# Half of the state groups in one recurrence, and all of its preparation on VectorE, in an MLA + S5 backbone

## The chip, the cores and the metric

The kernel runs on one core of a Trainium2 chip. The metric is the device time of one execution in microseconds (us). Five engines work side by side, each through its own list of instructions in order: TensorE (PE, with its weight loads PEld), VectorE (DVE), ScalarE (ACT), GpSimd (POOL) and SyncE (SP), which issues nearly all the DMAs.

## The reference, cut to what matters

Two post-norm layers over 512 latent tokens and 256 context tokens, 1024 features, float32. Layer 0 is latent attention and is not touched. Layer 1 is a bidirectional S5 state-space layer with a GLU:

```python
u_l, g_l = jnp.split(h_lat @ w_in, 2, axis=-1)      # also for the context
# per direction, per group (128 groups of 16 channels, 64 complex states):
#   state[t] = lam_bar * state[t-1] + b_bar u[t];   y[t] = Re(C state[t])
# first over the context, then, from its last state, over the latent tokens
y = jax.nn.gelu(d * u + y_forward + y_backward)
ya, yb = jnp.split(y @ w_glu + b_glu, 2, axis=-1)
out = ((ya * sigmoid(yb)) * silu(g)) @ w_out        # then residual and LayerNorm
```

## The kernel before, in words

Products with weights run as three float32r matmuls on parts: weights and inputs are split into a high part (`whi`, cast on ACT) and the rest (`wlo`, a subtraction on DVE, line 64).

Tokens are taken in chunks of 8: 64 chunks of latent tokens and 32 of context. Both directions of 64 states lie on the 128 partitions. Layer 1 has these stages, and `m` (0 to 15) counts pieces of 128 channels, which are 8 groups:

- **Stage A** (18 turns of the loop at line 1154). Turn t projects the channels of m = t (`u_tile`: 24 matmuls of 512 columns and 24 of 256), writes them to DRAM (`ud`) in one layout and reads them back in another (`u_load`). `s_tile(m)`, two turns later, makes each chunk's input to the state with 16 groups of matmuls of 96 columns, from weights `pt` (`win_chunk`). Of 32 pieces of such weights 24 were made ahead and are loaded; 8 late ones (pieces 5, 8, ... 26) are made here, by six operations on POOL (lines 372 to 377) out of two loads. ACT copies the results to `st` and, for the context, to `sc`. `tree(k)`, after every second m, folds the 32 context chunks of 16 groups into one state by five levels of four operations, on POOL (lines 1123 to 1128).
- **The recurrence** (`recur`, lines 1131 to 1142) turns inputs into states: 63 steps one after the other, each of four operations (lines 1138 to 1141) on all 32 groups of a quarter of the groups, that is 64 numbers a partition, each 256 bytes from the next. Three quarters run on DVE and the last one on POOL. A quarter can start when its two trees are done. `pull(n)` emits n steps of the recurrences that are open, between other work.
- **Stage B**: the gates (a projection, tanh and product, `gg`, stored to `gd`), and for each m `y_load` (state-out weights `wo`, lag table `toe`, `u`), `states` (copies of the states on ACT), `y_tile` (matmuls of 128 columns) and the copy `ot` on DVE. `gelu(n)` turns two of these and makes the GLU's inputs. y_tile(m) needs the finished recurrence of its groups.
- **GLU, output projection, norm**: matmuls in a row, with the weights loaded and split as they go.

What one writes down is not the order that the engines get: a scheduler of the framework places each engine's instructions. Each engine then runs its list in order, so an instruction that waits holds up all behind it. SP's list has the weight loads (`wraw`, which wait for the subtraction that frees their buffer), the loads of `pt`, `bt`, `u`, `toe`, `wo` and the stores of `gd` in one row.

Of the kernel before, what the change touches and what calls it, by code (L numbers as in the profile page):

```python
# [31 lines left out]
def hybrid_mla_s5(ctx, tc, I, O):  # L32
# [55 lines left out]
    def mod_steps(blocks, wt, ps, work, n):  # L88
        """rows of 512 columns of the modulation, block j in column group j: one step for each of the inputs' tiles"""
# [48 lines left out]
    def newton_rsqrt(y, t, ms):  # L138
        """y = 1/sqrt(ms), with one Newton step"""
        act.activation(y, ms, AF.Abs_reciprocal_sqrt)  # L140
        dve.tensor_mul(t, y, y)
        dve.tensor_mul(t, t, ms)
        dve.tensor_scalar(t, t, -0.5, 1.5, op0=ALU.mult, op1=ALU.add)
        dve.tensor_mul(y, y, t)
# [14 lines left out]
    def s5_params(take, mm):  # L159
# [102 lines left out]
        # (lam_bar - 1) / lam  # L262
# [16 lines left out]
        # powers: slot s holds lam_bar^s forward, lam_bar^(7-s) backward; state-in coefficients  # L279
        # coef * lam_bar * slot(7 - i), groups on the partitions, conjugated  # L280
# [33 lines left out]
    def s5_chunk(work, mm, c, pw, cci, half, dcol, eyek):  # L314
        """state-out weights and lag tables of groups 4c .. 4c+3"""
# [16 lines left out]
        # input weights of the lag table, the directions in separate columns  # L332
# [48 lines left out]
    def win_early(tables, scratch, engs, more):  # L381
        """pieces made ahead and kept in DRAM: the last one is stored, the next one loaded, this one made"""
# [13 lines left out]
    # ================= layer 0: latent attention =================  # L396
    with ExitStack() as ctx_:
# [25 lines left out]
        def turn_rows(dst, src):  # L423
            """the features that the rotation pairs: blocks of 16 rows change places"""
            for i in range(8):
                sp.dma_start(out=dst[16 * i:16 * i + 16, :], in_=src[16 * (i ^ 1):16 * (i ^ 1) + 16, :])

        def stack(src, dst0, dst1, sl):
            """hi and lo of two heads' 64 rope features, one over the other"""
# [77 lines left out]
        with mkpool(name="in_h", bufs=KC) as hp, mkpool(name="in_w", bufs=3) as wp, \  # L507
# [20 lines left out]
            def mod_part(q):  # L528
                """shift and scale of 256 features, the even and the odd tiles of the inputs apart"""
# [74 lines left out]
            def rms(tiles, cols, n):  # L604
                """RMSNorm over the partitions of the tiles, in place"""
# [86 lines left out]
            def mod_more():  # L692
                """a step of the products with the modulation weights, and the loads for the next one"""
# [19 lines left out]
        with mkpool(name="at_s", bufs=2) as work, mkpool(name="at_p", bufs=2, space=PSUM) as ps, \  # L713
# [7 lines left out]
            # a unit is 128 latent queries of a head, or its 256 context queries  # L721
# [36 lines left out]
            def turn(i):  # L758
                """probabilities with the keys on the partitions, split"""
# [51 lines left out]
            for i, (h, u) in enumerate(units + [(HEADS, 0), (HEADS, 0)]):  # L811
# [19 lines left out]
                if i == len(units) - 8:  # L831
                    # the first operands of the output projection
# [27 lines left out]
    def norm_cols(work, st):  # L860
        """mean and 1/std of rows from the statistics of their pieces"""
# [6 lines left out]
    # PSUM from here on: four tiles of a bank, and two of two banks  # L868
# [66 lines left out]
    def res_load(tt, n):  # L935
        """gate and residual of a token tile, for half of the features"""
# [35 lines left out]
    # the weights in the order of their use, 1024 columns at a time, two pieces ahead  # L972
# [25 lines left out]
    with mkpool(name="o_s", bufs=1, side="right") as work:  # L998
# [19 lines left out]
        def modulated(tt, z):  # L1018
            """input of layer 1, feature-major, split"""
# [29 lines left out]
    def win_chunk(c):  # L1049
# [6 lines left out]
        win_make(pool, pt, bt, *(winp.tile([P, 4, P], F32, name=f"t{i}", bufs=1) for i in range(2)))  # L1056

    # ================= layer 1: S5 =================
    ud = [dram.tile([8, P, 96], F32, name=f"ud{m}") for m in range(16)]
    gd = [dram.tile([P, TL], F32, name=f"gd{m}") for m in range(16)]  # L1060
    stes, (stp,) = pools(dict(name="st", bufs=4))
    ST = [stp.tile([P, 2, 32, 64], F32, name="st") for _ in range(4)]      # states: (re, -im), group, chunk
# [20 lines left out]
    def s_tile(m):  # L1083
        """state inputs of the groups of an m: in the order of each direction's steps"""
# [19 lines left out]
    def lam(l, gs, tail):  # L1104
        """the power's real part, and (+,-) its imaginary part, for (re, -im) states"""
# [7 lines left out]
    def tree(k):  # L1113
        """state after the context, for 16 groups"""
        x = scs.pop(k)
        gs = slice(16 * k, 16 * k + 16)
        for l in range(5):
# [5 lines left out]
            pool.tensor_tensor(a, ev, lr, op=ALU.mult)  # L1123
            pool.tensor_tensor(b, ev[:, ::-1], li, op=ALU.mult)
            pool.tensor_tensor(a, a, b, op=ALU.add)
            g = slice(16 * k % 32, 16 * k % 32 + 16)
            dst = a if l < 4 else ST[k // 2][:, :, g, 0:1]
            pool.tensor_tensor(dst, a, od, op=ALU.add)
            x = a

    def recur(q, work, eng):
        """states before each chunk of the latent tokens, for 32 groups, in steps"""
        st = ST[q]
        lr, li = lam(0, slice(32 * q, 32 * q + 32), 0)
        for k in range(63):
            t1 = work.tile([P, 2, 32], F32, name="rt1", bufs=4)
            t2 = work.tile([P, 2, 32], F32, name="rt2", bufs=4)
            eng.tensor_tensor(t1, st[:, :, :, k], lr, op=ALU.mult)  # L1138
            eng.tensor_tensor(t2, st[:, ::-1, :, k], li, op=ALU.mult)  # L1139
            eng.tensor_tensor(st[:, :, :, k + 1], st[:, :, :, k + 1], t1, op=ALU.add)  # L1140
            eng.tensor_tensor(st[:, :, :, k + 1], st[:, :, :, k + 1], t2, op=ALU.add)  # L1141
            yield
# [11 lines left out]
    for t in range(18):  # L1154
# [10 lines left out]
        if m >= 0:  # L1165
            s_tile(m)
            pull(3)
            if m % 2 == 1:
                tree(m // 2)
            if m % 4 == 3 and m < 15:  # L1170
                rec.append(recur(m // 4, stp, dve))
# [20 lines left out]
    yes, (ep,) = pools(dict(name="y_s", bufs=2, side="right"))  # L1192
    rec.append(recur(3, stp, pool))
    toe, ins = {}, {}

    def y_load(m):
# [5 lines left out]
        wo = [ep.tile([P, 4, 2, P], F32, name="wo", bufs=5) for _ in range(2)]  # L1202
        for c in range(2):
            sp.dma_start(out=wo[c], in_=wod[2 * m + c])
        u = ep.tile([P, 8, 96], F32, name="u", bufs=3)
# [5 lines left out]
    def states(m):  # L1211
        """the states of 8 groups; the backward half was made in the order of its steps: turn it round"""
# [5 lines left out]
    def y_tile(m):  # L1218
        """two groups at a time in the halves of the columns, chunks on the partitions"""
# [11 lines left out]
        if m % 2 == 0:  # L1231
            ot[m // 2] = ep.tile([P, 8, 2, 64], F32, name="ot")
# [5 lines left out]
    def gelu(n):  # L1238
        """channels of two tiles turned onto the partitions; tanh form, split"""
# [4 lines left out]
        for e in range(2):  # L1244
# [7 lines left out]
            h, l = (VV[v // 4][:, v % 4, i] for i in range(2))  # L1252
# [23 lines left out]
    gates(6, gg)  # L1276
    states(0)
    gates(1, gg)
    for m in range(16):
# [3 lines left out]
        pull(4)  # L1283
        if m < 15:
            states(m + 1)
        if "gggggggg.g.a.aaa"[m] == "g":
            gates(1, gg)
        elif "gggggggg.g.a.aaa"[m] == "a":
            glu_mm()
        if m % 4 == 2:  # L1290
            VV.append(stp.tile([P, 4, 2, TL], F32R, name="st"))
        if m % 4 >= 2:
            gelu(m // 2 - (m % 2 == 0))
# [26 lines left out]
    with mkpool(name="f_s", bufs=1, side="right") as work:  # L1320
# [25 lines left out]
        wlast = [stp.tile([P, 2, 2, D], F32R, name="st") for _ in range(4)]  # L1346
# [32 lines left out]
def tables():  # L1379
# [9 lines left out]
    cs = np.stack([cos, sin * sgn], 1)[tok]          # [512, 2, 64]  # L1389
# [4 lines left out]
def lay_out(inp):  # L1394
# [13 lines left out]
    def mtiles(w):                                     # [K, M] -> [M/128, 128 p, K/128 * 128]  # L1408
# [7 lines left out]
    uk, uv = g["mla_w_uk"][0], g["mla_w_uv"][0]        # [128 c, 16, 128]  # L1416
# [5 lines left out]
    def dp(a):                                         # [2, 128 g, 64 p, ...] -> [(d p), g, ...]  # L1422
# [48 lines left out]
```

## Time and profile before

| what | before |
|---|---|
| runs shown, us | 1840.08, 1853.53, 1857.38 |
| median | 1853.53 |
| span of the profiled execution | 1848.7 |
| PE busy / DVE busy / POOL busy in the span | 1653.3 / 1137.1 / 683.2 |
| TensorE clock granted, mean | 0.944 |

The page gives no time of the profiled execution beside its span; the span lies inside the three times. Starts are counted from the span's start. Layer 1's stage A takes about 962 to 1218 us, stage B 1218 to 1412, the rest the remaining 436 us.

### The profile page before, as it was taken

To read this page: it belongs to the slowest core of one execution; us is meant where nothing else is said; L and a number is where in the kernel's file an instruction comes from. 1 tells how busy PE (TensorE), PEld (TensorE's weight loads), DVE (VectorE), ACT (ScalarE), POOL (GpSimd) and SP (SyncE) were. 2 spreads that over 40 slices of the span, in tenths; PEclk is the share of its full clock that TensorE was granted. 3 is DMA by queue.
4 is the path that set the end of the run, shared out by engine and by line. 5 is a ranking of instruction groups with operands and counts; after the bars stand their busy time and mean duration, and the time that the engine had idled before them with its cause. 6 is when DMAs were issued, how large, how long until landed. Compare 5 with 4: busy or idle time off the path is not lost.

```text
span 1848.7 us, 26973 instructions
## 1 busy us (share of the span) xinstructions
PE 1653.3 (89%) x9754; PEld 1321.5 (71%) x9754; DVE 1137.1 (62%) x2356; ACT 694.6 (38%) x1415; POOL 683.2 (37%) x788
## 2 busy tenths in 40 slices
PE   7999998888988989987899875687979999999997
PEld 4755787766766767766779765565768888888876
DVE  3864448888899677735551499998844332333347
ACT  2511226465565646611334332233454222222220
POOL 0000017666776477445105664626770000000022
PEclk8999999899999989998999887888989999999999
DMA  9366412222222455467647755339995333333352
GB/s 324 99 211 203 112 52 88 74 92 83 85 70 90 136 164 166 145 204 219 202 133 211 165 134 153 119 91 266 258 288 156 129 108 105 112 98 119 105 180 68
DMA packets 144244, 268.82 MB, mean 145 GB/s; under 512 B 39760, under 2 KB 74848, under 8 KB 143984
## 3 DMA queue, kind: packets, MB, share of 16 engines
q1 hardware_dynamic: 126256, 258.69, 46.9%
q10 hardware_dynamic: 17792, 8.39, 1.6%
q8 instruction: 77, 1.26, 0.3%
q14 instruction: 55, 0.45, 0.1%
q0 software_dynamic: 64, 0.03, 0.0%
HBM read 215.39 MB, written 49.30 MB: 143 GB/s over the span
## 4 chain that ended last, share of the span: by engine, by line
PE 53%; DVE 21%; DMA 14%; ACT 3%; issue 3%; POOL 3%; SPq 1%; DVEq 0%; ACTq 0%; POOLq 0%
PE mm L80 13%; PE mm L81 13%; PE mm L82 13%; DMA wraw<-in_wout_dram 3%; DVE st L1141 3%; DVE rt L1138 3%; DMA pt<-pind 3%; DVE st L1140 2%; DVE rt L1139 2%; PE modps L102 2%; PE sc L739 2%; PE sc L738 2%; DVE wlo L64 2%; DMA toe<-kd 2%; PE tr L775 2%
## 5 line engine op out<-in xcount | busy, mean ns | idle before, releaser
L64 DVE TENSOR_TENSOR wlo<-wraw,whi 128x1024 fp32r<-128x1024 f32 (+1 forms) x155 | 184.2, 1190 | 349.1 <-ACT whi L64 347.8
L64 ACT CAST whi<-wraw 128x1024 fp32r<-128x1024 f32 (+1 forms) x155 | 148.9, 962 | 467.5 <-PE mm L81 302.9
L81 PE MATMUL mm<-st,whi 128*128 128x512 f32 x512 | 201.6, 394 | 0.0
L80 PE MATMUL mm<-st,whi 128*128 128x512 f32 x512 | 201.3, 393 | 0.4 <-DVE t L1250 0.4
L82 PE MATMUL mm<-st,wlo 128*128 128x512 f32 x512 | 198.9, 388 | 0.0
L1333 POOL TENSOR_TENSOR x<-x,row_g 128x1024 f32<-128x1024 f32 x4 | 9.6, 2402 | 426.2 <-DMA x<-x1d 387.1
L80 PE MATMUL mm<-h,whi 128*128 128x512 f32 (+1 forms) x384 | 142.7, 372 | 11.6 <-DVE gg L1178 7.1
L325 POOL TENSOR_TENSOR wt<-cb,pw 128x512 f32<-128x512 f32 x32 | 36.3, 1133 | 301.5 <-DVE mx L752 268.3
L82 PE MATMUL mm<-h,wlo 128*128 128x512 f32 (+1 forms) x384 | 140.1, 365 | 6.4 <-DVE wlo L64 6.4
L81 PE MATMUL mm<-h,whi 128*128 128x512 f32 (+1 forms) x384 | 140.2, 366 | 0.8 <-DVE h L1034 0.8
L1093 PE MATMUL mm<-u,pt 128*128 128x96 f32 x512 | 73.1, 307 | 54.9 <-DMA u<-ud 36.5
L80 PEld LDWEIGHTS mm<-st,whi 128*128 128x128 f32 x512 | 96.1, 188 | 23.6 <-PE mm L82 0.8
L1093 PEld LDWEIGHTS mm<-u,pt 128*128 128x128 f32 x512 | 70.0, 221 | 58.2 <-issue 34.6
L82 PEld LDWEIGHTS mm<-st,wlo 128*128 128x128 f32 x512 | 96.1, 188 | 21.5
L81 PE MATMUL mm<-hl,whi 128*128 128x512 f32 (+1 forms) x320 | 109.9, 345 | 0.4 <-DVE hl L570 0.4
L81 PEld LDWEIGHTS mm<-st,whi 128*128 128x128 f32 x512 | 96.3, 188 | 19.1
L80 PE MATMUL mm<-hh,whi 128*128 128x512 f32 (+1 forms) x320 | 108.2, 346 | 1.7 <-ACT whi L64 1.7
L82 PE MATMUL mm<-hh,wlo 128*128 128x512 f32 (+1 forms) x320 | 108.9, 344 | 0.2 <-DVE wlo L64 0.2
L372 POOL TENSOR_TENSOR t<-pt,bt 128x512 f32<-128x512 f32 x14 | 20.8, 1488 | 223.8 <-DMA pt<-pind 177.4
L749 DVE TENSOR_REDUCE mx<-sc 128x1 f32<-128x768 f32 (+1 forms) x96 | 74.0, 772 | 37.4 <-PE sc L739 37.3
L775 PE MATMUL tr<-ident,p 128*128 128x128 f32 x448 | 72.2, 283 | 26.3 <-DVE ptl L64 22.7
L80 PEld LDWEIGHTS mm<-h,whi 128*128 128x128 f32 x384 | 75.4, 197 | 24.3 <-DVE gg L1178 7.9
(350 smaller groups left out, 4532.8 us busy)
## 6 DMA issues: line engine op xcount, KB each, us to landing
wraw<-in_wglu_dram SPq DMA_DIRECT2D x64, 512.0 KB
wraw<-in_win_dram SPq DMA_DIRECT2D x52, 512.0 KB
wod<-wo SPq DMA_DIRECT2D x32, 512.0 KB
wo<-wod SPq DMA_DIRECT2D x32, 512.0 KB
pt<-wid SPq DMA_DIRECT2D x24, 512.0 KB
u<-ud SPq DMA_DIRECT2D x32, 384.0 KB
pt<-pind SPq DMA_DIRECT2D x18, 512.0 KB
bt<-in_Bc_dram SPq DMA_DIRECT2D x18, 512.0 KB
```

The source lines that it names most:

```text
L64: return act.copy(hi, src).ins, dve.tensor_sub(lo, src, f(hi)).ins
L80: pe.matmul(ps, lh, rh, start=first, stop=False)
L81: pe.matmul(ps, lh, rl, start=False, stop=False)
L82: pe.matmul(ps, ll, rh, start=False, stop=last)
L102: pe.matmul(mps[32 * j:32 * j + 2, :], sT[:, kc, :], w, start=(kc == 0), stop=(kc == KC - 1))
L738: pe.matmul(o, xr[half, ts], kh[half, a:b], start=False, stop=False)
L739: pe.matmul(o, xr[:, ts], kx[:, a:b], start=False, stop=True)
L749: dve.reduce_max(mx[:, 0:1], s, axis=AX.X)
L775: pe.transpose(tp[:, n, :], p[:, j * P:(j + 1) * P], ident)
L1093: pe.matmul(o[:, r, 96 * q:96 * (q + 1)], wi[:, q, r, :], us[m][:, 4 * (c % 2) + q, :], start=True, stop=True)
L1138: eng.tensor_tensor(t1, st[:, :, :, k], lr, op=ALU.mult)
L1141: eng.tensor_tensor(st[:, :, :, k + 1], st[:, :, :, k + 1], t2, op=ALU.add)
```

## The change

The recurrence runs over a half of the groups at a time (two instead of four, 128 numbers a partition and operation) and wholly on DVE; the trees and the eight late pieces of state-in weights move from POOL to DVE. The first half can start after m = 7, the second after m = 15. The states lie in two large tiles instead of four, so the GLU's inputs `VV` and the last weights `wlast` do too, and four results `ot` wait for a `gelu` of a half at once. Five gates instead of seven come ahead of the first y_tile, one more with each of the first 11. `wo` has 4 buffers instead of 5, `u` 2 instead of 3, the recurrence's scratch 2 instead of 4. Comments are dropped all over, which shifts line numbers by 2 to 5.

```diff
-        win_make(pool, pt, bt, *(winp.tile([P, 4, P], F32, name=f"t{i}", bufs=1) for i in range(2)))
+        win_make(dve, pt, bt, *(winp.tile([P, 4, P], F32, name=f"t{i}", bufs=1) for i in range(2)))
...
-    stes, (stp,) = pools(dict(name="st", bufs=4))
-    ST = [stp.tile([P, 2, 32, 64], F32, name="st") for _ in range(4)]      # states: (re, -im), group, chunk
+    stes, (stp,) = pools(dict(name="st", bufs=2))
+    SH = [stp.tile([P, 2, 2, 32, 64], F32, name="st") for _ in range(2)]
+    ST = [SH[q // 2][:, q % 2] for q in range(4)]
...
-            pool.tensor_tensor(a, ev, lr, op=ALU.mult)
-            pool.tensor_tensor(b, ev[:, ::-1], li, op=ALU.mult)
-            pool.tensor_tensor(a, a, b, op=ALU.add)
+            dve.tensor_tensor(a, ev, lr, op=ALU.mult)
+            dve.tensor_tensor(b, ev[:, ::-1], li, op=ALU.mult)
+            dve.tensor_tensor(a, a, b, op=ALU.add)
...
-            pool.tensor_tensor(dst, a, od, op=ALU.add)
+            dve.tensor_tensor(dst, a, od, op=ALU.add)
...
-    def recur(q, work, eng):
-        st = ST[q]
-        lr, li = lam(0, slice(32 * q, 32 * q + 32), 0)
+    def recur(h, work):
+        st = SH[h]
+        gs = slice(64 * h, 64 * h + 64)
+        lr = lamt[:, 0, 0, gs].rearrange("p (q g) -> p q g", q=2).unsqueeze(2).broadcast_to([P, 2, 2, 32])
+        li = lamt[:, 0, 1:3, gs].rearrange("p r (q g) -> p q r g", q=2)
         for k in range(63):
-            t1 = work.tile([P, 2, 32], F32, name="rt1", bufs=4)
-            t2 = work.tile([P, 2, 32], F32, name="rt2", bufs=4)
-            eng.tensor_tensor(t1, st[:, :, :, k], lr, op=ALU.mult)
...
+            t1 = work.tile([P, 2, 2, 32], F32, name="rt1", bufs=2)
+            t2 = work.tile([P, 2, 2, 32], F32, name="rt2", bufs=2)
+            dve.tensor_tensor(t1, st[:, :, :, :, k], lr, op=ALU.mult)
+            dve.tensor_tensor(t2, st[:, :, ::-1, :, k], li, op=ALU.mult)
+            dve.tensor_tensor(st[:, :, :, :, k + 1], st[:, :, :, :, k + 1], t1, op=ALU.add)
+            dve.tensor_tensor(st[:, :, :, :, k + 1], st[:, :, :, :, k + 1], t2, op=ALU.add)
...
-            if m % 4 == 3 and m < 15:
-                rec.append(recur(m // 4, stp, dve))
+            if m % 8 == 7:
+                rec.append(recur(m // 8, stp))
...
-    rec.append(recur(3, stp, pool))
...
-        wo = [ep.tile([P, 4, 2, P], F32, name="wo", bufs=5) for _ in range(2)]
+        wo = [ep.tile([P, 4, 2, P], F32, name="wo", bufs=4) for _ in range(2)]
...
-        u = ep.tile([P, 8, 96], F32, name="u", bufs=3)
+        u = ep.tile([P, 8, 96], F32, name="u")
...
-    gates(6, gg)
+    gates(4, gg)
     states(0)
     gates(1, gg)
+    gelus = {6: (0, 1), 7: (2,), 8: (3,), 14: (4, 5), 15: (6, 7)}
     for m in range(16):
...
-        pull(4)
+        pull(6)
...
-        if "gggggggg.g.a.aaa"[m] == "g":
+        if "ggggggggggg.aaaa"[m] == "g":
...
-        if m % 4 == 2:
-            VV.append(stp.tile([P, 4, 2, TL], F32R, name="st"))
-        if m % 4 >= 2:
-            gelu(m // 2 - (m % 2 == 0))
+        if m in (6, 14):
+            VV.append(stp.tile([P, 8, 2, TL], F32R, name="st"))
+        for n in gelus.get(m, ()):
+            gelu(n)
...
-        wlast = [stp.tile([P, 2, 2, D], F32R, name="st") for _ in range(4)]
+        wlast = [t[:, i] for t in [stp.tile([P, 2, 2, 2, D], F32R, name="st") for _ in range(2)] for i in range(2)]
```

What the scheduler makes of it shows on DVE. First DVE's list before, in the middle of stage A: between two weight subtractions (L64) stand recurrence operations only.

```order
L64 TENSOR_TENSOR wlo<-wraw,whi 128x1024
L1140 TENSOR_TENSOR st<-st,rt_11287 128x64
L1141 TENSOR_TENSOR st<-st,rt_11288 128x64
L1138 TENSOR_TENSOR rt_11293<-st,lamt 128x64
L1139 TENSOR_TENSOR rt_11294<-st,lamt 128x64
L1140 TENSOR_TENSOR st<-st,rt_11293 128x64
L1141 TENSOR_TENSOR st<-st,rt_11294 128x64
```

The same stretch of DVE's list in the change, while the first half's recurrence (L1142 to L1145) runs; L1126 to L1130 are the tree of m = 8 and 9, L372 to L377 make state-in weights out of the loads `pt` and `bt`.

```order
L1126 TENSOR_TENSOR trb<-tr_11384,lamt 128x32x8
L1144 TENSOR_TENSOR st<-st,rt_11202 128x128
L372 TENSOR_TENSOR t_11149<-pt,bt 128x512
L373 TENSOR_TENSOR t_11150<-pt,bt 128x512
L1127 TENSOR_TENSOR tr_11390<-tr_11390,trb 128x256
L1145 TENSOR_TENSOR st<-st,rt_11203 128x128
L374 TENSOR_TENSOR bt<-pt,bt 128x4x128
L375 TENSOR_TENSOR bt<-pt,bt 128x4x128
L1130 TENSOR_TENSOR tr_11390<-tr_11390,tr_11384 128x256
L1142 TENSOR_TENSOR rt_11208<-st,lamt 128x128
L1143 TENSOR_TENSOR rt_11209<-st,lamt 128x128
L64 TENSOR_TENSOR wlo<-wraw,whi 128x1024
```

So tree, weights, recurrence and weight subtraction now follow one another in one list: from the start of the first half's recurrence to the end of the second's it holds 504 recurrence operations, 4 trees, 3 pieces of weights, 20 subtractions, 15 gate products, 8 `ot` copies and 22 operations of the GELU.

The second place is the end of that list's recurrence, in stage B. Behind the last step come the GELU's and the `ot` copies (L1236) of m = 8 on.

```order
L1142 TENSOR_TENSOR rt_13088<-st,lamt 128x128
L1143 TENSOR_TENSOR rt_13089<-st,lamt 128x128
L1251 SCALAR_TENSOR_TENSOR t<-t,mm_13502 128x512
L1144 TENSOR_TENSOR st<-st,rt_13088 128x128
L1145 TENSOR_TENSOR st<-st,rt_13089 128x128
L1253 SCALAR_TENSOR_TENSOR t<-t,mm_13502 128x512
L76 SCALAR_TENSOR_TENSOR st<-t,st 128x512
L1236 COPY ot<-mm 128x4x8x16 x2
```

Before, the last step on DVE belonged to the third quarter (m = 8 to 11), and the fourth ended on POOL; now m = 8 and m = 15 wait for the same step.

## Rows read from the trace of the kernel before

**Rows 1.** Stretches: us, busy of PE, PEld, DVE, ACT, POOL, clock, DMA share, GB/s

```profile
962.00:1071.00 109.00, 101.34 (x652) 92.53 (x652) 36.83 (x64) 47.45 (x93) 66.24 (x77) 0.94 0.72 188
1071.00:1218.00 147.00, 99.73 (x584) 89.69 (x583) 142.36 (x414) 44.81 (x86) 79.43 (x113) 0.80 0.44 130
1218.00:1340.00 122.00, 97.92 (x670) 80.37 (x670) 110.89 (x340) 43.67 (x53) 76.01 (x185) 0.90 0.88 220
1340.00:1412.00 72.00, 61.44 (x569) 52.41 (x566) 32.30 (x45) 38.02 (x51) 34.21 (x88) 0.91 0.99 267
1412.00:1848.00 436.00, 424.37 (x1855) 346.87 (x1853) 167.03 (x189) 104.51 (x121) 22.78 (x8) 0.99 0.34 112
```

**Rows 2.** Waits of PE, 958 to 1218 us: total, times, longest

```profile
PE mm L1093 <- DMA u<-ud: 36.5, 6, 15.3
PE mm L1093 <- POOL pt L376: 15.4, 3, 9.5
```

**Rows 3.** Waits of SP's queue, 1071 to 1346 us: total, times, longest

```profile
SPq L983 <- DVE st L1140: 59.7, 8, 17.1
```

**Rows 4.** Timeline of VectorE, a step with GpSimd idle: start, duration

```profile
1073.62 0.27 DVE L1138 TENSOR_TENSOR rt<-st,lamt 128x64 f32<-128x64 f32 x1
1073.81 0.26 DVE L1139 TENSOR_TENSOR rt<-st,lamt 128x64 f32<-128x64 f32 x1
...
1074.29 0.28 DVE L1141 TENSOR_TENSOR st<-st,rt 128x64 f32<-128x64 f32 x1
1074.61 0.27 DVE L1138 TENSOR_TENSOR rt<-st,lamt 128x64 f32<-128x64 f32 x1
```

**Rows 5.** Timeline of VectorE, one operation with GpSimd busy

```profile
1057.44 1.38 DVE L1140 TENSOR_TENSOR st<-st,rt 128x64 f32<-128x64 f32 x1
```

**Rows 6.** Timeline of GpSimd at the same time

```profile
1057.40 1.29 POOL L1125 TENSOR_TENSOR tr<-tr,trb 128x512 f32<-128x512 f32 x1
```

**Rows 7.** VectorE's groups of instructions: count | busy, mean ns | idle before

```profile
L1141 DVE TENSOR_TENSOR st<-st,rt 128x64 f32<-128x64 f32 x189 | 71.3, 392 | 4.1
L1140 DVE TENSOR_TENSOR st<-st,rt 128x64 f32<-128x64 f32 x189 | 68.1, 374 | 0.0
L1138 DVE TENSOR_TENSOR rt<-st,lamt 128x64 f32<-128x64 f32 x189 | 66.9, 354 | 10.4 <-POOL st L1128 5.6
L1139 DVE TENSOR_TENSOR rt<-st,lamt 128x64 f32<-128x64 f32 x189 | 64.4, 341 | 0.0
```

**Rows 8.** The same view: rows of adjacent numbers, 128 and 32 a partition

```profile
L241 DVE TENSOR_TENSOR G<-G 128x128 f32<-128x128 f32 x21 | 6.1, 290 | 29.2 <-PE mm L297 28.8
L121 DVE TENSOR_TENSOR modc<-mm,bmod 128x32 f32<-128x32 f32 x1 | 0.2, 182 | 0.0
```

**Rows 9.** Timeline of VectorE: an early piece of weights, made there

```profile
836.69 0.69 DVE L372 TENSOR_TENSOR t<-pt,bt 128x512 f32<-128x512 f32 x1 [4.33 <-DMA pt<-pind]
837.30 0.68 DVE L373 TENSOR_TENSOR t<-pt,bt 128x512 f32<-128x512 f32 x1
...
839.84 0.68 DVE L377 TENSOR_TENSOR pt<-bt 128x512 f32<-128x512 f32 x1
```

**Rows 10.** Timeline of ScalarE: two turns of stage A, and s_tile(7)'s last copy

```profile
1049.66 0.59 ACT L1075 COPY ub<-mm 128x512 f32<-128x512 f32 x1 [4.26 <-PE mm L82]
1061.61 0.59 ACT L1075 COPY ub<-mm 128x512 f32<-128x512 f32 x1 [3.44 <-PE mm L82]
...
1070.31 0.37 ACT L1102 COPY sc<-mm 64x256 f32<-64x256 f32 x1
```

**Rows 11.** Timeline of VectorE: the copies of y_tile(8) and y_tile(15)

```profile
1358.32 0.69 DVE L1233 COPY ot<-mm 128x512 f32<-128x512 f32 x1 [0.43 <-PE mm L1230]
...
1411.81 0.68 DVE L1233 COPY ot<-mm 128x512 f32<-128x512 f32 x1
```

**Rows 12.** DMA queues, 1243 to 1412 us: packets, MB, share of 16 engines

```profile
q1 hardware_dynamic: 28840, 44.28, 101.7%
```

**Rows 13.** GpSimd's groups, 1071 to 1340 us, as rows 7

```profile
L372 POOL TENSOR_TENSOR t<-pt,bt 128x512 f32<-128x512 f32 x4 | 5.2, 1289 | 39.4 <-DMA pt<-pind 29.6 <-DMA bt<-in_Bc_dram 9.8
```

More of the change, by code (lines that the diff above doesn't have):

```diff
@@ L1122, in tree @@
             ev, od = x[:, :, :, 0::2], x[:, :, :, 1::2]
-            pool.tensor_tensor(a, ev, lr, op=ALU.mult)
-            pool.tensor_tensor(b, ev[:, ::-1], li, op=ALU.mult)
-            pool.tensor_tensor(a, a, b, op=ALU.add)
+            dve.tensor_tensor(a, ev, lr, op=ALU.mult)
+            dve.tensor_tensor(b, ev[:, ::-1], li, op=ALU.mult)
+            dve.tensor_tensor(a, a, b, op=ALU.add)
             g = slice(16 * k % 32, 16 * k % 32 + 16)
             dst = a if l < 4 else ST[k // 2][:, :, g, 0:1]
-            pool.tensor_tensor(dst, a, od, op=ALU.add)
+            dve.tensor_tensor(dst, a, od, op=ALU.add)
             x = a
-    def recur(q, work, eng):
-        st = ST[q]
-        lr, li = lam(0, slice(32 * q, 32 * q + 32), 0)
-        for k in range(63):
-            t1 = work.tile([P, 2, 32], F32, name="rt1", bufs=4)
-            t2 = work.tile([P, 2, 32], F32, name="rt2", bufs=4)
-            eng.tensor_tensor(t1, st[:, :, :, k], lr, op=ALU.mult)
-            eng.tensor_tensor(t2, st[:, ::-1, :, k], li, op=ALU.mult)
-            eng.tensor_tensor(st[:, :, :, k + 1], st[:, :, :, k + 1], t1, op=ALU.add)
-            eng.tensor_tensor(st[:, :, :, k + 1], st[:, :, :, k + 1], t2, op=ALU.add)
+    def recur(h, work):
[3 more added lines that the diff above has]
+        li = lamt[:, 0, 1:3, gs].rearrange("p r (q g) -> p q r g", q=2)
+        for k in range(63):
+            t1 = work.tile([P, 2, 2, 32], F32, name="rt1", bufs=2)
[4 more added lines that the diff above has]
+            dve.tensor_tensor(st[:, :, :, :, k + 1], st[:, :, :, :, k + 1], t2, op=ALU.add)
             yield
@@ L1231, in y_tile @@
         if m % 2 == 0:
-            ot[m // 2] = ep.tile([P, 8, 2, 64], F32, name="ot")
+            ot[m // 2] = ep.tile([P, 8, 2, 64], F32, name="ot", bufs=4)
         dve.tensor_copy(ot[m // 2][:, :, m % 2, :].rearrange("p j (g c) -> p g j c", c=16),
@@ L1251, in gelu @@
             v = 2 * n + e
-            h, l = (VV[v // 4][:, v % 4, i] for i in range(2))
+            h, l = (VV[v // 8][:, v % 8, i] for i in range(2))
             half_split(t, *(x.rearrange("p (j k) -> p j k", k=64) for x in (h, l)))
@@ L1282, in hybrid_mla_s5 @@
             y_load(m + 2)
-        pull(4)
+        pull(6)
         if m < 15:
             states(m + 1)
-        if "gggggggg.g.a.aaa"[m] == "g":
+        if "ggggggggggg.aaaa"[m] == "g":
             gates(1, gg)
-        elif "gggggggg.g.a.aaa"[m] == "a":
+        elif "ggggggggggg.aaaa"[m] == "a":
             glu_mm()
-        if m % 4 == 2:
-            VV.append(stp.tile([P, 4, 2, TL], F32R, name="st"))
-        if m % 4 >= 2:
-            gelu(m // 2 - (m % 2 == 0))
+        if m in (6, 14):
+            VV.append(stp.tile([P, 8, 2, TL], F32R, name="st"))
+        for n in gelus.get(m, ()):
+            gelu(n)
     wdma[0] = sp
```

## The prediction

> **What bounds the kernel now.** I read the time slices first, to see where PE is not busy: layer 0 and the GLU keep it full, so what can be won lies in layer 1's state-space stages. Then the stretches [rows 1]. From 1071 to 1218 us, the second part of stage A, PE works 99.7 of 147 us at a granted clock of 0.80 (its upper level, 2.4 GHz, only part of the time), while DVE is busy 142.4 of them. From 1218 to 1340 DVE has 110.9 of 122. From 1340 to 1412 neither is full, but the DMA engines are (0.99).
>
> Next, who waits for whom. PE names loads of `u` (36.5 us) and POOL's late weights (15.4 us) [rows 2], not DVE. But `u` stands in SP's list behind weight loads that wait for a buffer, and these wait for DVE: the entry of 59.7 us names a recurrence operation ahead of the subtraction that frees the buffer [rows 3]. So DVE's list sets the pace of stage A through SP's.
>
> Last, why DVE is full. A step of the recurrence with POOL idle takes 0.99 us (1073.62 to 1074.61) for four operations of 0.26 to 0.28 us [rows 4]. With POOL in a long operation the same operation takes 1.38 us [rows 5], and it ends as POOL's ends [rows 6]. Over the kernel the four groups take 270.7 us for 189 steps [rows 7], 1.43 us a step. At 0.99 they would take 187: about 84 us of DVE's time go to this overlap.
>
> **What the change removes.** All POOL work in these stages, and so the overlap. Also 63 of DVE's 189 steps, since it now makes 126.
>
> **What it adds to DVE, step by step.**
> - *A step of 128 numbers.* Operations of 512 adjacent numbers follow one another every 0.61 us [rows 9], of 64 every 0.19 [rows 4]: 0.94 ns a number, so 64 more cost 0.06, four times 0.24, and the step 1.23 us. But 64 numbers in adjacent places should last 0.22 us, between the 0.18 of 32 and the 0.29 of 128 [rows 8]; the recurrence's last 0.27. Its numbers lie 256 bytes apart, and no row shows 128 of those. If the 0.05 extra is per operation, the step stays 1.23; if it is per number, it doubles and the step is 1.43. Nothing excludes either, so I take the middle, 1.33: 126 steps are 168 us (ends 155 and 180).
> - The Trainium skill speaks for the upper end ("SBUF — State Buffer", section "Door 1: The DMA port swizzle"): SBUF is read in lines of 16 bytes, and an access that crosses to a new line pays. The rows agree that such operations cost more. By that rule a half at a time wins little over two quarters (1.43 against 1.98).
> - *A tree.* Five levels of 512, 256, 128, 64 and 32 numbers: 0.61 + 0.37 + 0.25 + 0.19 + 0.16 = 1.58 by the same line, four operations each, 6.3 us; three of four wait for the one before, which costs 0.13 more (0.32 from 1074.29 to 1074.61, against 0.19, [rows 4]), 15 times: 1.9. Together 8 us, times eight.
> - *A late piece of weights.* From 836.69 to about 840.5: 3.8 us [rows 9], where POOL needs six times 1.3 [rows 13] and more for the tree operations between.
>
> **The sum.** The first half's recurrence starts when tree 3 is done. s_tile(7) ended at 1070.3 [rows 10]. Pieces 8, 11 and 14 become 4 us shorter each, in a chain through the one `bt` buffer; PE's own turn takes 12 us (1049.66 to 1061.61, [rows 10]) and the loads stay, so of 12 us I give half: 1064 (ends 1058 and 1070). With tree 3 the start is 1072.
>
> From there to the last step of the second half, DVE's list holds (counts in the section on the change): 126 steps, 168; 4 trees, 32; 3 pieces, 11; 20 subtractions of 1024 numbers at 1.1, 22; 45 operations of 512 at 0.61, 27. That is 260 us. DVE was idle 3% of its fullest stretch [rows 1], so 268: the recurrence ends at 1340.
>
> y_tile(8) follows it. Its copy was at 1358 before, the one of y_tile(15) at 1412, 53.5 us later [rows 11]. With two sets of `wo` and `u` only m = 8 and 9 are loaded while PE waits. Still to come are six sets of 1.44 MB, two `toe` of 1.05 and two weights of 0.52: 11.8 MB. From 1243 to 1412 the queue moved 44.28 MB in 169 us with all engines taken [rows 12], 0.262 MB a us: 45 us, and some 9 for the first and the last tile. So y_tile(15)'s copy comes at 1340 + 54 = 1394 instead of 1412: **18 us less**.
>
> Before that, loads don't bind: m = 0 to 9 and the gates' weights are some 30 MB, 115 us at that rate, and can start when the gates do, near 1190. Nor does PE: from 1218 to 1340 it was busy 97.9 us with the gates and seven tiles [rows 1]; begun near 1170, as much is done near 1270.
>
> At nothing I cost: the gates' spread and the GELU of a half at once, since y_tile(15) comes behind the same three GLU pieces as before, and five more of the eight that need only the first half (120 matmuls at 424.37 / 1855 = 0.229 us, [rows 1], 27 us of PE) cover the last GELUs; without that cover up to those 27 would show. Two large tiles for the last weights: the first half of the output projection covers their splits. The scratch of two, on one engine in order. SP's reload of `lamt`, which now waits for the last step and stands ahead of the `wo` of m = 10: those wait for y_tile(8) anyway.
>
> The sum is against the profiled span of 1848.7 us, which gives 1831; the median shown is 4.8 above that span, and 18 off it is **1836 us**.
>
> **Rivals.**
> 1. *The light end.* The step costs 1.23, and s_tile(7) comes at 1058: start 1066, plus 92 + 155 without idle time, ends at 1313; 1367 for y_tile(15), 45 less: **1809**. For it: the prices of adjacent numbers, and 84 us of overlap that goes. Against: waits for `u` of up to 15.3 us in stage A [rows 2], which no faster DVE removes by itself.
> 2. *The heavy step*, 1.43 as if each strided number paid: 12 more, **1848**. For it: the operations of 64 are already dearer than adjacent ones. It is the result that the line rule of the Trainium skill's SBUF page gives; no row of 128 bears it out yet.
> 3. *Slower: the late weights wait at the head of DVE's list.* On POOL a piece waited for its two loads, 39.4 us over four of them [rows 13], and nothing else stood behind. On DVE the recurrence and the subtractions do, and through these SP's loads. Three pieces lie inside the chain above; at 10 us each, with the heavy step, 42 are added to it, 24 more than the gain: **1877**. It outweighs the gain from 18 us on and is slower by 1% from 37. Against it: by the prices above the list has about 14 us of other work between one piece and the next, in which the loads run.
> 4. *The overlap isn't POOL's doing*, so that the change does not free DVE. Then a step is 1.43 + 0.24 and the 126 cost 42 more: 24 slower, **1877** too. Against it: the DVE and the POOL operation of [rows 5, 6] end together (1058.8 and 1058.7), and steps at 0.99 are those beside an idle POOL.
>
> **Chances.** Forecast 0.30, rival 1 0.28, rival 2 0.19, rival 3 0.17, rival 4 0.04, a gain still larger 0.02. About 1%, 18.5 us, is what a measurement of this kernel can tell from no change. The forecast lies on that bound and is split: faster 0.28 + 0.02 + 0.15 = 0.45; same 0.15 + 0.19 = 0.34; slower 0.21. The range takes in rival 1 and goes into rival 3 to its half: 1805 to 1868.
>
> **What would show it.** Steps right: POOL nearly idle from 980 to 1400; the four recurrence operations near 0.3 us each without long ones, 1.2 to 1.45 us a step; the recurrence's last step 15 us or less from 1340; then about 54 us to y_tile(15). Wrong would be: idle time of DVE in front of L372 above 15 us after the recurrence starts; a step above 1.5; PE held by `wo` or `u` before y_tile(8), which would mean that loads bind earlier than I say; or a y_tile(15) that follows the last step much sooner than 54 us.

## The result, and the profile after

The changed kernel takes 1863.95 us (median of 7 runs, 1861.2 to 1872.7), the kernel before 1846.35 (7 runs, 1840.08 to 1857.38): a ratio of 1.0076, 95% interval 1.0052 to 1.0100. It is slower by 0.8%, about 14 us, where I forecast 18 us less. The profiled execution spans 1862.4 us, against 1848.7.

First the stretches of the changed kernel, columns as in [rows 1].

```profile
962.00:1071.00 109.00, 106.81 (x702) 98.36 (x701) 50.28 (x102) 48.77 (x95) 0.00 (x0) 0.97 0.75 202
1071.00:1218.00 147.00, 113.35 (x621) 99.55 (x620) 133.35 (x365) 49.45 (x91) 0.00 (x0) 0.85 0.67 174
1218.00:1340.00 122.00, 88.06 (x633) 70.20 (x632) 117.37 (x293) 41.02 (x51) 0.00 (x0) 0.87 0.80 199
1340.00:1412.00 72.00, 51.62 (x448) 43.30 (x448) 26.68 (x50) 29.47 (x34) 0.00 (x0) 0.79 0.66 183
1412.00:1862.00 450.00, 432.19 (x1900) 351.45 (x1898) 170.90 (x198) 109.63 (x129) 22.92 (x8) 0.98 0.33 109
```

POOL is idle, as forecast, and PE does more in stage A (106.8 and 113.4 us instead of 101.3 and 99.7). But DVE is as full as before: 133.4 of 147 us, then 117.4 of 122 (142.4 and 110.9 in [rows 1]). Its groups of instructions over the kernel, columns as in [rows 7], say why.

```profile
L1145 DVE TENSOR_TENSOR st<-st,rt 128x128 f32<-128x128 f32 x126 | 53.7, 427 | 3.1
L1144 DVE TENSOR_TENSOR st<-st,rt 128x128 f32<-128x128 f32 x126 | 52.8, 420 | 0.0
L1142 DVE TENSOR_TENSOR rt<-st,lamt 128x128 f32<-128x128 f32 x126 | 47.4, 376 | 3.1
L1143 DVE TENSOR_TENSOR rt<-st,lamt 128x128 f32<-128x128 f32 x126 | 46.4, 369 | 0.0
...
L372 DVE TENSOR_TENSOR t<-pt,bt 128x512 f32<-128x512 f32 x12 | 10.3, 858 | 71.1 <-DMA pt<-pind 67.3 <-DMA bt<-in_Bc_dram 3.8
```

The long operations of [rows 5] are gone: the means are close to what a single operation takes now. But that is 0.37 to 0.43 us for 128 numbers. Four of them make a step of 1.45 us (1199.91 to 1201.36 in the timeline: start, duration):

```profile
1199.91 0.37 DVE L1142 TENSOR_TENSOR rt<-st,lamt 128x128 f32<-128x128 f32 x1
1200.20 0.36 DVE L1143 TENSOR_TENSOR rt<-st,lamt 128x128 f32<-128x128 f32 x1
1200.47 0.40 DVE L1144 TENSOR_TENSOR st<-st,rt 128x128 f32<-128x128 f32 x1
1200.91 0.41 DVE L1145 TENSOR_TENSOR st<-st,rt 128x128 f32<-128x128 f32 x1
1201.36 0.37 DVE L1142 TENSOR_TENSOR rt<-st,lamt 128x128 f32<-128x128 f32 x1
```

In the same timeline the last step of the recurrence, the copies of y_tile(8) and y_tile(15) stand so:

```profile
1351.72 0.42 DVE L1145 TENSOR_TENSOR st<-st,rt 128x128 f32<-128x128 f32 x1
...
1359.34 0.69 DVE L1236 COPY ot<-mm 128x512 f32<-128x512 f32 x1 [1.57 <-PE mm L1233]
...
1414.54 0.69 DVE L1236 COPY ot<-mm 128x512 f32<-128x512 f32 x1 [0.37 <-PE mm L1233]
```

The last step ends at 1352.1, the copy of y_tile(15) comes 62.4 us later, 2.7 us behind that of before [rows 11]. From there to the end the changed kernel needs 447.9 us (1862.4 less 1414.5), the kernel before 436.9 (1848.7 less 1411.8). So most of the 13.7 us between the spans lies behind y_tile(15). The 86 us behind it, first of the changed kernel, then of the kernel before:

```profile
1414.00:1500.00 86.00, 80.20 (x351) 64.11 (x348) 34.55 (x42) 27.80 (x37) 0.00 (x0) 0.96 0.29 94
```

```profile
1412.00:1498.00 86.00, 85.62 (x379) 70.07 (x378) 33.58 (x38) 26.27 (x33) 0.00 (x0) 1.00 0.33 107
```

PE is idle for 5.8 us of these, not 0.4, and its clock is 0.96 of the upper level, not 1.00. PE's timeline in the changed kernel shows what it waited for: the products of the last GELUs.

```profile
1437.35 1.03 PE L1246 MATMUL mm<-ident,ot 128*128 128x128 f32 x8
...
1441.84 0.80 PE L80 MATMUL mm<-st,whi 128*128 128x512 f32 x1 [2.76 <-ACT st L75]
...
1445.40 0.77 PE L80 MATMUL mm<-st,whi 128*128 128x512 f32 x1 [1.61 <-DVE t L1253]
```

### The profile page after: what moved, and what is told of

It is laid out like the page before. It is cut to its first block, busy times and chain, and to the rows that moved or that the text cites. A ratio compares the mean times of both kernels' runs of the same rounds, so it can differ in the third digit from the quotient of the medians.

```text
span 1862.4 us, 26437 instructions
## 1 busy us (share of the span) xinstructions
PE 1664.3 (89%) x9754; PEld 1327.0 (71%) x9754; DVE 1151.8 (62%) x2312; ACT 697.0 (37%) x1415; POOL 426.3 (23%) x328
## 5 line engine op out<-in xcount | busy, mean ns | idle before, releaser
L64 DVE TENSOR_TENSOR wlo<-wraw,whi 128x1024 fp32r<-128x1024 f32 (+1 forms) x155 | 180.9, 1171 | 284.6 <-ACT whi L64 283.4
L64 ACT CAST whi<-wraw 128x1024 fp32r<-128x1024 f32 (+1 forms) x155 | 149.2, 964 | 461.9 <-PE mm L81 318.0
L80 PE MATMUL mm<-whi,vh 128*128 128x512 f32 x186 | 72.9, 416 | 18.0 <-ACT whi L64 15.5
L64 DVE TENSOR_TENSOR ptl<-tr,pth 128x384 fp32r<-128x384 f32 (+1 forms) x160 | 80.0, 521 | 10.8 <-ACT pth L64 10.2
L80 PEld LDWEIGHTS mm<-h,whi 128*128 128x128 f32 x384 | 74.6, 195 | 16.6 <-DVE gg L1182 4.6
L81 PEld LDWEIGHTS mm<-h,whi 128*128 128x128 f32 x384 | 74.7, 195 | 11.8 <-DVE h L1034 1.1
```

The source lines that it names most:

```text
L64: return act.copy(hi, src).ins, dve.tensor_sub(lo, src, f(hi)).ins
L80: pe.matmul(ps, lh, rh, start=first, stop=False)
L81: pe.matmul(ps, lh, rl, start=False, stop=False)
```

## The experiments

Ratios are to the kernel before, run on the same chip, with their 95% intervals; where two edited kernels are compared, I divide their ratios, because the kernel before itself had medians from 1846 to 1856 us. Starts and ends are those of one profiled execution of each kernel.

### 1. The states with the groups innermost

The distance of 256 bytes between the recurrence's numbers is taken away.

```diff
-    SH = [stp.tile([P, 2, 2, 32, 64], F32, name="st") for _ in range(2)]
-    ST = [SH[q // 2][:, q % 2] for q in range(4)]
+    SH = [stp.tile([P, 64, 2, 2, 32], F32, name="st") for _ in range(2)]
+    ST = [SH[q // 2][:, :, q % 2].rearrange("p k r g -> p r g k") for q in range(4)]
...
-            dve.tensor_tensor(t1, st[:, :, :, :, k], lr, op=ALU.mult)
+            dve.tensor_tensor(t1, st[:, k], lr, op=ALU.mult)
```

> The changed kernel with one edit: the states lie with the groups innermost (128 adjacent numbers for a chunk instead of 128 numbers 256 bytes apart). Theory 'distance' (each number 256 bytes from the next costs the recurrence time of its own): the four operations go from 0.37 to 0.43 us to about 0.29, a step from 1.46 to 1.05 to 1.15, the last step comes some 40 us earlier (near 1312 instead of 1352); the loads of stage B then bind, so of 40 us I expect 20 to 30 in the time: about 1838. Rival 'step is latency' (the operation's cost is fixed and the dependence between the four makes it): step stays at 1.4 to 1.46, time stays at 1864. ACT's copies of states now write and read 512 bytes apart and may get longer; ACT was busy 49 of 147 us in the second part of stage A.

Measured: 1839.73 us, ratio 0.9948 (0.9919 to 0.9976), 1.3% below the changed kernel. DVE's groups:

```profile
L1142 DVE TENSOR_TENSOR rt<-st,lamt 128x128 f32<-128x128 f32 x126 | 36.7, 291 | 3.0
L1145 DVE TENSOR_TENSOR st<-st,rt 128x128 f32<-128x128 f32 x126 | 36.6, 291 | 3.1
```

The operations take 0.29 us, the step 1.06 (1133.06 to 1134.12), and the recurrence ends at 1318.2, 34 us earlier. The price of the changed kernel's step was the distance, not a fixed latency. Not all of it comes back: 126 steps of 0.39 us less would be 49 us, but from the first step (1069.7, 8 us earlier) to the last it is 248.5 us instead of 274.0. DVE's list now waits 15.3 us for ScalarE's part of the gates, 12.3 for loads of `pt` and 9.6 for ScalarE's `whi`. ScalarE pays for the new layout. Its groups in stages A and B (962 to 1412 us), of the changed kernel and of this one:

```profile
L1101 ACT COPY st<-mm 64x504 f32<-64x504 f32 x32 | 18.4, 574 | 28.1 <-PE mm L1095 26.4 <-ACT ub L1078 1.3
L1218 ACT COPY sm<-st 64x1024 f32<-64x1024 f32 x16 | 16.7, 1046 | 25.6 <-PE mm L1233 22.5 <-DVE st L1145 3.1
```

```profile
L1101 ACT COPY st<-mm 64x504 f32<-64x504 f32 x32 | 33.8, 1056 | 11.7 <-PE mm L1095 8.7 <-ACT ub L1078 2.7
L1218 ACT COPY sm<-st 64x1024 f32<-64x1024 f32 x16 | 32.1, 2006 | 12.1 <-PE mm L1233 9.8 <-DVE st L1145 2.2
```

Writing the state inputs 512 bytes apart, and reading the states so, takes about twice as long. ScalarE has the room for it (busy 73 of 147 us, then 68 of 122), though y_tile(8)'s copy now starts 9.1 us behind the last step instead of 7.2.

### 2. Runs of 4 and of 2 adjacent numbers

```diff
-    SH = [stp.tile([P, 2, 2, 32, 64], F32, name="st") for _ in range(2)]
+    SH = [stp.tile([P, 2, 16, 64, 4], F32, name="st") for _ in range(2)]    # runs of 2: [P, 2, 32, 64, 2]
```

> The changed kernel with the states in runs of 4 adjacent numbers (16 bytes) instead of single numbers 256 bytes apart; a chunk's 128 numbers are 32 such runs, 1024 bytes apart. If the price goes with the pieces (by lines of 16 bytes, or by every jump), a quarter of it is left: operations of 0.29 + 0.13 / 4 = 0.32 us, a step of 1.15, time 1840 to 1846. If it goes with each number that lies in a place of its own row of chunks, whatever its neighbours, operations stay at 0.37 to 0.43 and the time at 1864.

> The changed kernel with the states in runs of 2 adjacent numbers (8 bytes). Operations of 128 numbers take 0.37 to 0.43 us as single numbers and 0.285 to 0.29 both in runs of 4 and all adjacent. By lines of 16 bytes, each line touched costing something, 64 lines: 0.31 to 0.34. By a limit that hides under the pace of adjacent numbers: 0.29 as well. By a price for every jump the run of 4 would have shown some already; it did not, so 0.35 would speak for another rule.

Measured: runs of 4 give 1848.53 us, ratio 0.9959 (0.9938 to 0.9980), with operations of 0.285 to 0.290. That is less than the 0.32 us that I gave, and yet the time lies above the 1840 to 1846 that went with it. Runs of 2, one execution, 1841.74 us, have the same:

```profile
L1147 DVE TENSOR_TENSOR rt<-st,lamt 128x128 f32<-128x128 f32 x126 | 36.6, 290 | 3.1
...
L1148 DVE TENSOR_TENSOR rt<-st,lamt 128x128 f32<-128x128 f32 x126 | 35.8, 284 | 0.0
```

So a pair of adjacent numbers is enough; the price is neither one for each jump nor one for each line. The Trainium skill ("SBUF — State Buffer", section "Door 1: The DMA port swizzle (why `[64,N]` ≈ `[32,N]`)") says of its lines of 16 bytes that two accesses to a line are needed to hide the memory's latency. These runs agree: two in a line cost nothing here, one does.

Nor need the two be neighbours. The trees read every second number, 8 bytes apart, so that two of them lie in 16 bytes. First such an operation of 128 numbers in the changed kernel, then ScalarE in the runs of 2, where it writes and reads numbers 8 bytes apart (the last line writes adjacent ones):

```profile
L1130 DVE TENSOR_TENSOR tr<-tr,tr 128x128 f32<-128x128 f32 x8 | 2.3, 286 | 0.1
```

```profile
L1104 ACT COPY st<-mm 64x252 f32<-64x252 f32 x64 | 24.6, 384 | 12.8 <-PE mm L1095 9.0 <-ACT ub L1078 3.1
L1225 ACT COPY sm<-st 64x512 f32<-64x512 f32 x32 | 21.1, 659 | 24.0 <-PE mm L1240 21.3 <-DVE st L1150 2.2
...
L1106 ACT COPY sc<-mm 64x256 f32<-64x256 f32 x32 | 11.7, 366 | 0.4
```

DVE takes the 0.29 us of adjacent numbers, and ScalarE 0.384 us for 252, near the 0.366 of 256 adjacent ones. Distances between 8 and 16 bytes were not tried.

### 3. ScalarE writes runs of 4

Runs of 4 with ScalarE going through a run first, and the edit of experiment 4.

```diff
-            act.copy(st[lo_, :, c % 8, 1:64].rearrange("p r k g -> p r g k"), o[lo_, :, :, 0:63])
+            act.copy(st[lo_, :, c % 8, 1:64], o[lo_, :, :, 0:63].rearrange("p r g k -> p r k g"))
```

> States in runs of 4 adjacent numbers, with ScalarE's copies of the state inputs going through the 4 of a run first, and the GLU input in the projection's place. If ScalarE too pays for single numbers that lie apart when it writes them, its copy of 504 numbers falls from 1.07 us to about 0.6 although it now reads apart; if reading apart costs the same, it stays at 1.07. On the time: ScalarE is not the bound, so as the groups-innermost kernel with the same second edit, ratio to the kernel before 0.986 to 0.993.

Measured: 1839.6 us, ratio 0.9934 (0.9908 to 0.9959), no better than experiment 9, the groups-innermost kernel with the same second edit. The copies, in ScalarE's groups:

```profile
L1223 ACT COPY sm<-st 64x512 f32<-64x512 f32 x32 | 36.3, 1134 | 0.4
...
L1101 ACT COPY st<-mm 64x504 f32<-64x504 f32 x32 | 18.3, 573 | 18.9 <-PE mm L1095 17.3 <-ACT ub L1078 1.3
```

The write of 504 numbers is back at 0.57 us though it reads PSUM 384 bytes apart; the copy of states, which still reads single numbers 16 bytes apart, stays at 1.12 to 1.13 for 512. ScalarE's 32 us less on the writes (64 copies, 0.5 us each; the copies of states take 8 us more than in experiment 9) bring no time.

### 4. The second GLU input where the projection's input was

```diff
-    gelus = {6: (0, 1), 7: (2,), 8: (3,), 14: (4, 5), 15: (6, 7)}
+    gelus = {6: (0, 1), 7: (2,), 8: (3,), 11: (4,), 12: (5,), 13: (6,), 15: (7,)}
...
-        if m in (6, 14):
+        if m == 6:
             VV.append(stp.tile([P, 8, 2, TL], F32R, name="st"))
+        if m == 11:
+            VV.append(h1p.tile([P, 8, 2, TL], F32R, name="h1"))
...
-    ZZ = [h1p.tile([P, 8, 2, TL], F32R, name="h1"), ...
+    ZZ = [stp.tile([P, 8, 2, TL], F32R, name="st"), ...
```

> The changed kernel with one edit: the GLU's second input tile lies where the projection's input was (free after the last gate), so that GELUs 4 to 6 run right behind their y_tiles (at m = 11, 12, 13) and only GELU 7 behind m = 15, as before. Theory 'four GELUs in a row at the end are not covered': from the last copy ot to the end 448 us go back to 437, the time falls by 8 to 11 us to about 1855. Rival 'the end waits for weight loads or the clock': tail stays 446 to 448, time 1862 to 1866.

Measured: 1854.6 us, ratio 1.0021 (0.9990 to 1.0052), 0.55% or 10 us below the changed kernel. The span is 1844.3 us; DVE's timeline has y_tile(15)'s copy, and the stretch behind it has PE nearly without a gap at full clock:

```profile
1405.69 0.68 DVE L1236 COPY ot<-mm 128x512 f32<-128x512 f32 x1
```

```profile
1406.00:1492.00 86.00, 84.56 (x374) 69.09 (x373) 33.20 (x39) 26.88 (x34) 0.00 (x0) 1.00 0.31 105
```

From that copy to the end it is 438.6 us instead of 447.9. The same edit on the groups-innermost kernel (experiments 1 and 9) has the same: from copies at 1381.35 and 1389.35 to spans of 1829.3 and 1827.9 it is 448.0 us without it and 438.6 with it. So the GELUs that wait for the half's tile cost 9 to 10 us there. In runs of 4 they cost less: the same stretch is 443.2 us without the edit (experiment 2) and 438.6 with it (experiment 3). The profiled execution of this kernel is the quickest of its ten, and its y_tile(15) also comes 8.9 us earlier than in the changed kernel; that part is not shown to come from the edit.

### 5 and 6. The preparation alone, and the halves alone

The kernel before with the trees and the late weights on DVE; and the changed kernel with both back on POOL.

```diff
 # the kernel before, preparation on DVE
-        win_make(pool, pt, bt, ...
+        win_make(dve, pt, bt, ...
-            pool.tensor_tensor(a, ev, lr, op=ALU.mult)      # and so for the whole tree
+            dve.tensor_tensor(a, ev, lr, op=ALU.mult)
 # the changed kernel, preparation on POOL: the same lines the other way round
```

> The kernel before with only the preparation moved: trees and late state-in weights on VectorE, recurrence in quarters as before (the fourth on GpSimd). Theory 'the overlap with GpSimd stretched the recurrence': with GpSimd idle until its quarter starts, VectorE's steps of 64 numbers fall from a mean of 1.43 to 1.0 to 1.1 us; the fourth quarter on GpSimd (it took some 100 us) and the loads of stage B then set the end: 1835 to 1850. Rival 'late weights hold VectorE's list' (their two loads are waited for at the head of it): idle time in front of the first operation of a piece above 40 us in all while recurrences are open, time 1855 to 1880.

> The changed kernel with the trees and the late weights put back on GpSimd; halves, GELU and gates as changed. Theory 'overlap': an operation of 128 numbers beside a GpSimd operation lasts 1.2 to 1.4 us like one of 64, so while GpSimd works (some 80 us of the stretch 1078 to 1218) steps take over 2 us; the mean step rises to 1.6 or more and the time to 1870 to 1890. Rival 'preparation on VectorE costs as much as it saves': VectorE loses 32 + 11 us of work and its waits for loads, the last step comes no later than 1352, time 1850 to 1864.

Measured: the preparation alone makes the kernel before faster, 1844.12 us, ratio 0.9959 (0.9932 to 0.9986). The halves alone make it slower, 1881.75 us, 1.0167 (1.0112 to 1.0222). Two of the four groups of DVE in the first:

```profile
L1141 DVE TENSOR_TENSOR st<-st,rt 128x64 f32<-128x64 f32 x189 | 54.1, 293 | 3.0
...
L1138 DVE TENSOR_TENSOR rt<-st,lamt 128x64 f32<-128x64 f32 x189 | 50.4, 267 | 4.3
```

The four sum to 211 us instead of the 270.7 of [rows 7]. And in the second, where POOL is busy 99 us between 1071 and 1218:

```profile
L1145 DVE TENSOR_TENSOR st<-st,rt 128x128 f32<-128x128 f32 x126 | 60.6, 482 | 3.6
L1142 DVE TENSOR_TENSOR rt<-st,lamt 128x128 f32<-128x128 f32 x126 | 54.9, 436 | 12.7 <-POOL st L1130 9.1
```

Here each operation is some 0.06 us dearer in the mean than without POOL's work, the first step starts at 1107.5 instead of 1078.1, and the last ends at 1376.9 instead of 1352.1. So the overlap with POOL is real in both directions. The Trainium skill ("SBUF — State Buffer", section "Who interferes with whom") has a rule for it: an operation of VectorE with two inputs in SBUF contends with one of GpSimd that reads SBUF. The runs agree (270.7 us beside GpSimd's work, 211 without most of it). But the time of the second kernel, which I forecast from it, has another cause in the main: from its first step to its last it is 269.4 us, 5 less than in the changed kernel, with trees and weights off DVE's list. What is late is its start, by 29 us: it follows the fourth tree, which POOL ends at 1107.4. My rival 3, late weights at the head of DVE's list, did not come while recurrences ran: DVE's waits for their loads, first in 900 to 1078 us of the changed kernel, then in 1078 to 1352 (total, times, longest), are

```profile
DVE t L372 <- DMA pt<-pind: 51.5, 5, 13.3
```

```profile
DVE t L372 <- DMA pt<-pind: 8.5, 2, 4.6
```

The 51.5 us lie ahead of the recurrence's first step.

### 7. Two sets of buffers in the kernel before

```diff
-        wo = [ep.tile([P, 4, 2, P], F32, name="wo", bufs=5) for _ in range(2)]
+        wo = [ep.tile([P, 4, 2, P], F32, name="wo", bufs=4) for _ in range(2)]
-        u = ep.tile([P, 8, 96], F32, name="u", bufs=3)
+        u = ep.tile([P, 8, 96], F32, name="u")
```

> The kernel before with the changed kernel's buffers alone: two sets of state-out weights and of u (4 and 2 buffers) instead of two and a half and three (5 and 3). In the changed kernel the DMA engines were full from 1360 to 1402 with two sets, so by the theory that the loads' rate and not the buffers set the end there, this alone changes nothing: ratio to the kernel before 0.997 to 1.003. Rival: with fewer buffers the loads of m = 8 to 15 start later and wait for each y_tile, 5 to 10 us: ratio 1.003 to 1.006.

Measured: 1860.65 us, ratio 1.0043 (1.0016 to 1.0070). The rival held. Copies of y_tile(8) and y_tile(15) on DVE:

```profile
1357.89 0.68 DVE L1233 COPY ot<-mm 128x512 f32<-128x512 f32 x1
...
1422.33 0.68 DVE L1233 COPY ot<-mm 128x512 f32<-128x512 f32 x1
```

y_tile(8) comes as before, y_tile(15) 64.4 us behind it instead of 53.5. The smaller buffers alone cost the kernel before 3 to 13 us. What they cost in the changed kernel was not tried.

### 8. The last tree on POOL

PE waits 22.6 us at the start of stage B in the changed kernel (1184.6 to 1207.2). The view names DVE's L1145 as what ended it, but the matmuls that wait read `toe` and `u`, which are loads; they are issued at 1192.1. I took the last tree to hold them, since it ends then and its scratch lies in their place.

```diff
-        x = scs.pop(k)
+        x, eng = scs.pop(k), pool if k == 7 else dve
```

> The changed kernel with the last tree alone on GpSimd. In the changed kernel this tree ends at 1192.1 among steps of the recurrence, and stage B's first loads are issued then, since they lie in the place of its scratch; PE waits 22.6 us for them. On GpSimd it should end near 1182. Theory 'VectorE's list sets the end': loads and PE's wait move forward by some 10 us, the last step stays at 1348 to 1356 and the time at 1860 to 1866. Rival 'this wait of PE sets the end': time 1852 to 1856.

Measured: 1866.72 us, ratio 1.0060 (1.0033 to 1.0086), as the changed kernel. The tree ends on POOL at 1186.2, but SP issues its loads (`toe`) at 1193.5, behind a weight load and a gate's store:

```profile
1192.15 0.33 SPq L983 DMA_DIRECT2D wraw<-in_win_dram  x1
1193.09 0.32 SPq L1183 DMA_DIRECT2D gd<-gg  x1
1193.51 4.04 SPq L1204 DMA_DIRECT2D toe<-kd  x8
```

In the changed kernel it is the same: the loads follow a gate's store without a gap, and their issue at 1192.10 starts before the tree's last operation has ended (1191.93 and 0.21 us).

```profile
1191.73 0.32 SPq L1183 DMA_DIRECT2D gd<-gg  x1
1192.10 4.08 SPq L1204 DMA_DIRECT2D toe<-kd  x8
```

```profile
1191.93 0.21 DVE L1130 TENSOR_TENSOR st<-tr,tr 128x32 f32<-128x32 f32 x1
```

So these loads come at their place in SP's list, behind a weight load and a store that wait for DVE, and no wait for the tree shows. Since neither they nor the last step (it ends at 1353.0) moved, the run doesn't tell its two theories apart.

### 9 to 11. Together

> The groups-innermost states and the second GLU input tile in the projection's place, both in the changed kernel. If the two losses are separate, they add: 24 us and 9 us below the changed kernel's 1864, so 1828 to 1834, and below the kernel before. If the loads of stage B bind once the recurrence is short, the second edit is hidden: 1836 to 1842.

> Groups innermost, the GLU input in the projection's place, and the last tree on GpSimd. With cheap steps VectorE was busy 86 of 122 us in 1218 to 1340, and its list waits for PE's products, so here PE's wait for stage B's first loads should count: 8 to 10 us below the kernel without the last edit, 1818 to 1824. If loads in the rest of stage B bind instead, no difference to it.

> Groups innermost and the GLU input in the projection's place, and seven gates instead of five ahead of the first y_tile (the loop's last two gates move there). PE waits 18.9 us for stage B's first loads in the kernel without this edit; two gates are 48 matmuls, 11 us. If that hole costs time, the kernel gains 5 to 10 us on it (ratio to the kernel before 0.984 to 0.987). Rival: the second half's last step still comes when VectorE's list lets it, so the time that the gates fill there is missing between y_tile(7) and y_tile(8): no change, ratio 0.987 to 0.992.

Measured: the edits of experiments 1 and 4 together 1837.88 us, ratio **0.9893** (0.9860 to 0.9927): 1.8% below the changed kernel, 1.1% below the kernel before. The 1837.88 us lie where I put the case of a hidden second edit, but the kernel before took 1856.34 us beside it and 1852.07 beside experiments 1 and 4. By the ratios the second edit adds 0.55% to the first, as it does alone. The last tree on POOL adds nothing (0.9893, 0.9852 to 0.9934); seven early gates (`gates(6, gg)` for `gates(4, gg)`) are no better (0.9931, 0.9900 to 0.9963), with the last step ending at 1337.3 instead of 1327.6.

## Why the prediction was wrong

Against the profiled spans I was 31 us too low: 1831 for 1862.4. By its own steps, read from the one profiled execution:

- **Start of the first half**: 1072 forecast, 1078.1 measured. 6 us. In experiment 4, whose edit lies behind it, it is 1072.6, so these 6 us are not shown to be an error of the sum.
- **DVE's list to the last step**: 268 forecast, 274 measured. The step cost 1.45 instead of 1.33: 126 steps, 183 us instead of 168, above even the upper end of 180. The step is the mis-sized term, 15 us. Only 6 of them show, because all else, forecast at 92 and 8 idle, took 91 with its idle 12. I took the middle between "per operation" and "per number", and it is per number, as the line rule that I set beside it would have it for numbers this far apart. Experiments 1 and 2 show it; they also show that pairs pay nothing, which the rule as I put it does not say.
- **From the last step to y_tile(15)**: 54 forecast, 62.4 measured. From y_tile(8)'s copy it was 55.2, so the loads were sized about right. I had put y_tile(8) at the last step itself; it needs the copy of its states and its matmuls first, 7.2 us (1352.1 to 1359.3). This is read from the trace, not tried.
- **The GELU of a half at once, costed at nothing**: 11 us (447.9 for 436.9 behind y_tile(15)), 9 to 10 of them shown by experiment 4. I counted the GLU pieces that cover these GELUs, but four GELUs were left behind y_tile(14), not two, each a chain between DVE and ACT through one `t` buffer.

6 + 6 + 8 + 11 are the 31 us. The step and the GELUs are the two terms that failed and that experiments show. With the heavy step alone I had 1848 (rival 2); the GELUs and the way from the last step to y_tile(8) stood in no case. Right were the idle POOL, the end of the long operations and what bounds the chain. Rival 3 was wrong: in front of L372 DVE stood idle 8.5 us once the recurrence ran. Rival 4 was wrong: POOL is what stretched DVE's operations. But my 84 us for this were too many: operations that follow one another overlap (0.27 us long, the next one 0.19 behind, [rows 4]), so the durations of [rows 7] sum to more than the steps take. Like against like, experiment 5 shows 60 (270.7 and 211).

One sign of being wrong did come: PE stood 22.6 us ahead of y_tile(0), before its loads of `toe` and `u`. No run shows that it set the last step: DVE waited for something in only 12 of the 274 us.

What stays is why so large a change moved so little. The preparation on DVE is worth 0.4% (experiment 5), and the halves on top of it cost 1.2% (1.0076 against 0.9959). DVE gains nothing by the halves: 126 steps of 1.45 us are 183 us, and 189 steps at the 0.99 of [rows 4] are 187. One step of 128 is a good deal cheaper than two of 64 (1.98; I called that little), but DVE now also does the quarter that was POOL's, and while each number paid for its place the two came out even. The loss lies behind that: of the 17 us between the profiled executions of experiment 5's first kernel and the changed one, 10 lie behind y_tile(15)'s copy (1407.68 to 1845.4 is 437.7 us, against 447.9), where the GELUs are (0.55%). Two sets of buffers cost 0.43% in the kernel before. How far these parts add up inside the changed kernel was not tried.

## What to carry to other kernels

Before joining short operations to save their fixed cost, look at how far apart their numbers lie: here one number alone in its place made the joined operation 30 to 50% dearer, and two adjacent ones cost no more than a row without gaps. Then follow what the larger grain delays: the last consumers (here GELUs) move together to the end, where nothing covers them, and their larger tiles are paid with buffers elsewhere.

## What the runs showed of the hardware that was not expected

- DVE, 128 numbers of 4 bytes: 0.285 to 0.29 us adjacent, in runs of 4 and in runs of 2; as single numbers 256 bytes apart 0.37 where one input lies so, 0.42 to 0.43 where an input and the output do. Every second number (8 bytes apart) costs no more than adjacent ones: 0.286 in the trees.
- ACT pays more: 504 numbers written 512 bytes apart 1.06 us instead of 0.575, 1024 read so 2.0 instead of 1.045; even single numbers 16 bytes apart cost it as much (1.07 to write 504 in the runs of 4 of experiment 2), and 8 bytes apart hardly anything (0.384 for 252, 0.366 for 256 adjacent). Reading PSUM 384 bytes apart cost nothing (0.573).
